# The final norm of the first 704 tokens: token tiles by transposes, or feature rows as they lie

## The chip, the cores and the metric

The kernel runs on one core of a Trainium2 chip. The metric is the device time of one execution in microseconds (us); the kernel before has a median of 1601.08 us over 3 runs (1600.66 to 1601.70).

## The reference

One layer of a streaming encoder on 1,024 prompt tokens and 32 sample tokens of 1,024 features: attention and an mLSTM, a merge, an output projection, a SwiGLU FFN, then the final norm. Only its end matters here:

```python
def rmsnorm(x, g):
    xf = x.astype(jnp.float32)
    y = xf * lax.rsqrt(jnp.mean(xf * xf, axis=-1, keepdims=True) + EPS)
    return (y * g.astype(jnp.float32)).astype(x.dtype)
...
    g, up = jnp.split(h2 @ w_gate_up, 2, axis=-1)
    x = x + gt2 * ((jax.nn.silu(g) * up) @ w_down)
...
    y_prompt = rmsnorm(xp, g_final)
    y_sample = rmsnorm(xs, g_final)
```

## The kernel before, in words

All 1,056 tokens (1,024 and 32) are treated together, with features on partitions and tokens along the free dimension, in three tiles of 352 tokens. The residual `x2[j]` (j = 0 to 7) holds 128 features of all tokens; `cut` = 704 is where the third tile begins. TensorE multiplies in split precision: each weight and each activation is a high and a low part (`split_to`: ScalarE copies the high part, line 409, VectorE or GpSimd subtracts to get the low part, line 410), and every product takes three matmuls (`PASSES`).

The down projection of the FFN comes last. For the first 704 tokens it is finished first, by direct products and a seven-product scheme (line 2057 and `times`, line 1811); its sums lie in `cs[0]` to `cs[7]`. What follows is the loop over j at the end of the kernel: for each j the down projection of the third tile, 22 pieces k in three blocks of 8, 8 and 6, three matmuls for each k, so 66 matmuls (line 2214) in one PSUM bank; then VectorE adds the result to `x2[j][:, 704:]` (line 2224).

The weights come through `Weights`: three raw buffers filled by DMA on SyncE's queue (line 419), and four split buffers `wsp` of 4 pieces each. When TensorE starts a block, the split of the next block is issued; its ScalarE copy waits until TensorE has left the buffer it goes to. The pieces of the third tile are split the same way from `sl` buffers (`split`, issued by `beside` and, where j = 0 needs them, in the loop itself), the last ones while j = 0 runs.

Beside the loop runs a side job, the generator `finish_some`: `Side.tick` is called after every second k, and takes 15 steps over 75 ticks; before j = 7 the job is drained. Its first eight steps add the branch to the residual of the first 704 tokens (VectorE, line 2186, 128x704 each). Then come six token tiles (five of 128 tokens and one of 64), `Finish`: eight TensorE transposes into two PSUM banks (line 2118), two ScalarE squares with a row sum (line 2119), three small GpSimd operations for the inverse root (lines 2126 to 2128), two VectorE multiplications by the inverse root and the gain row `gB` out of PSUM (line 2134), and two DMAs (line 2138) that store 128x512 each.

The last 352 tokens are `End`: three token tiles (128, 128 and 96). `End.ahead` transposes j = 0 to 6 inside j = 7, and `End.last` the remaining one behind it, scales, and stores the left half from ScalarE's queue and the right half from SyncE's. The third tile holds 64 prompt tokens and 32 sample tokens, which go to two outputs, so it takes two DMAs on each queue (line 2182).

The order on TensorE, ScalarE, VectorE and GpSimd is the order in which the program issues the instructions; each engine works through its own list. A scheduler places only SyncE's DMAs.

Of the kernel before, what the change touches and what calls it, by code (L numbers as in the profile page):

```python
# [8 lines left out]
F32 = mybir.dt.float32  # L9
F32R = mybir.dt.float32r  # L10
BF16 = mybir.dt.bfloat16
AF = mybir.ActivationFunctionType
# [127 lines left out]
def hybrid_stream_step(  # L140
# [3 lines left out]
    params, c_rows, w_ada, w_mod, w_in, b_if, rel_row, w_br_att, w_br_mlstm, w_out, w_gate_up, w_down, g_final,  # L144
    y_prompt, y_sample, new_k_p, new_v_p, new_conv_p, new_C_p, new_n_p, new_m_p,
# [1954 lines left out]
    class Finish:  # L2100


        def __init__(self, a, b):
            self.a, self.b, self.py = a, b, (bank(512), bank(512))
            self.st = sl_pool[0].tile([P, 4], F32, tag="fst", name=nm("fst"), bufs=4)
            self.y = tmpt((P, D))
            self.parts = 0

        def take(self, j0, j1):

            n = self.b - self.a
            for h in range(2):
                a, b = max(j0, 4 * h), min(j1, 4 * h + 4)
                if a >= b:
                    continue
                py = self.py[h]
                for j in range(a, b):
                    pe.transpose(py[:n, (j - 4 * h) * P:(j - 4 * h + 1) * P], x2[j][:, self.a:self.b], ident)
                act.activation(self.y[:n, a * P:b * P], py[:n, (a - 4 * h) * P:(b - 4 * h) * P], AF.Square,  # L2119
                               accum_out=self.st[:n, self.parts:self.parts + 1])  # L2120
                self.parts += 1

        def scale(self):
            n, st = self.b - self.a, self.st
            for i in range(1, self.parts):
                pool.tensor_tensor(st[:n, 0:1], st[:n, 0:1], st[:n, i:i + 1], op=ALU.add)  # L2126
            pool.tensor_scalar(st[:n, 0:1], st[:n, 0:1], 1.0 / D, EPS, op0=ALU.mult, op1=ALU.add)
            pool.tensor_tensor(st[:n, 3:4], st[:n, 0:1], mhalf[:n, 0:1], op=ALU.pow)

        def put(self):  # L2130
            n, y = self.b - self.a, self.y
            for h in range(2):
                cs = slice(h * 512, (h + 1) * 512)
                dve.scalar_tensor_tensor(y[:n, cs], self.py[h][:n], self.st[:n, 3:4], gB[:n, cs],
                                         op0=ALU.mult, op1=ALU.mult)
                for q, u, v in col_segments(self.a, self.b):
                    out = y_sample[0, u - S:v - S] if q else y_prompt[0, u:v]
                    sp.dma_start(out[:, cs], y[u - self.a:v - self.a, cs])

    class End:  # L2140
# [28 lines left out]
        def last(self):  # L2169
# [5 lines left out]
            for i, (y, py, (a, b)) in enumerate(zip(self.ys, self.py, self.cuts)):  # L2175
# [3 lines left out]
                for eng, cs in ((act, slice(0, 512)), (sp, slice(512, D))):  # L2179
                    for q, u, v in col_segments(a, b):  # L2180
                        out = y_sample[0, u - S:v - S] if q else y_prompt[0, u:v]
                        eng.dma_start(out[:, cs], y[u - a:v - a, cs])

    def finish_some(ranges):
        for j in range(KD):
            dve.scalar_tensor_tensor(x2[j][:, :cut], cs[j], gt2[:, 0, j:j + 1], x2[j][:, :cut],
                                     op0=ALU.mult, op1=ALU.add)
            yield
        last = None
        for a, b in ranges:  # L2190
            x = Finish(a, b)
            x.take(0, KD)
            x.scale()
            if last:
                last.put()
            last = x
            yield
        last.put()
# [83 lines left out]
```

## Time and profile before

| | |
|---|---|
| median of 3 runs | 1601.08 us |
| the profiled execution's own time | 1600.87 us |
| its span in the trace | 1598.5 us |
| instructions in the span | 27336 |
| busy: TensorE, VectorE, ScalarE, GpSimd | 98%, 70%, 50%, 26% |
| stores of the six token tiles (line 2138) | 12 DMAs of 256 KB, the last issued at 1575.6 us |

The span is what the trace covers; the execution's time is 2.37 us longer. In the profile, PE is TensorE's matmuls, PEld its weight loads, DVE VectorE, ACT ScalarE, POOL GpSimd, SPq and ACTq the DMA queues of SyncE and ScalarE; L2214 is line 2214 of the kernel. The chain of waits is followed back from the last instruction: its rows have a start, a duration, and the engine that was worked on or waited for. Rows of the timeline have a start, a duration, engine, line, operation and tiles, and in brackets the idle time ahead and what ended it.

### The profile page before, as it was taken

To read this page: it belongs to the slowest core of one execution; us is meant where nothing else is said; L and a number is where in the kernel's file an instruction comes from. 1 tells how busy PE (TensorE), PEld (TensorE's weight loads), DVE (VectorE), ACT (ScalarE), POOL (GpSimd) and SP (SyncE) were. 2 spreads that over 40 slices of the span, in tenths; PEclk is the share of its full clock that TensorE was granted. 3 is DMA by queue.
4 is the path that set the end of the run, shared out by engine and by line. 5 is a ranking of instruction groups with operands and counts; after the bars stand their busy time and mean duration, and the time that the engine had idled before them with its cause. 6 is when DMAs were issued, how large, how long until landed. Compare 5 with 4: busy or idle time off the path is not lost.

```text
span 1598.5 us, 27336 instructions
## 1 busy us (share of the span) xinstructions
PE 1569.2 (98%) x10197; PEld 1549.3 (97%) x10197; DVE 1122.9 (70%) x2285; ACT 791.3 (50%) x1749; POOL 423.3 (26%) x450
## 2 busy tenths in 40 slices
PE   7999999999999999999999999999999999999997
PEld 6999999999999999999999999999999999999997
DVE  7766555556766845546655699898898986799754
ACT  3665463544555545444434655544445444544443
POOL 1343242433223311000012100675565650000001
PEclk9999999999999999999999999999999999999999
DMA  9823223343132332775453311223222237427454
GB/s 362 268 81 97 94 83 108 91 137 109 36 97 65 87 86 87 127 257 174 130 152 113 96 55 59 89 67 105 70 88 86 68 94 240 136 80 251 137 153 127
DMA packets 209906, 193.48 MB, mean 121 GB/s; under 512 B 11483, under 2 KB 179071, under 8 KB 208751
## 3 DMA queue, kind: packets, MB, share of 16 engines
q1 hardware_dynamic: 207214, 189.92, 38.7%
q10 hardware_dynamic: 2528, 1.77, 0.4%
q8 instruction: 80, 1.31, 0.4%
q14 instruction: 52, 0.42, 0.1%
q0 software_dynamic: 32, 0.06, 0.0%
HBM read 153.24 MB, written 41.63 MB: 122 GB/s over the span
## 4 chain that ended last, share of the span: by engine, by line
PE 91%; DVE 3%; DMA 2%; ACT 2%; issue 1%; SPq 0%; POOL 0%; ACTq 0%; DVEq 0%; POOLq 0%
PE mm L443 41%; PE psb L1811 18%; PE mm L1811 10%; PE mm L2214 3%; PE mm L878 3%; PE psb L2214 2%; PE psV L783 2%; PE psb L2057 2%; PE psS L725 2%; DMA s<-in_w_ada_dram 1%; PE psT L752 1%; PE mm L2057 1%; DMA t<-in_x_sample_dram 1%; PE psV L1112 1%; PE mm L475 1%
## 5 line engine op out<-in xcount | busy, mean ns | idle before, releaser
L443 PE MATMUL mm<-s,wsp 128*128 128x352 f32 x4104 | 687.0, 324 | 0.1
L443 PEld LDWEIGHTS mm<-s,wsp 128*128 128x128 f32 x4104 | 657.3, 188 | 1.8 <-issue 0.4
L410 DVE TENSOR_TENSOR wsp<-wraw,wsp 128x512 fp32r<-128x512 f32 (+1 forms) x280 | 235.6, 858 | 127.4 <-ACT wsp L409 125.3
L1811 PE MATMUL psb<-s,wsp 128*128 128x352 f32 x1611 | 271.7, 322 | 1.6 <-DVE wsp L410 0.9
L409 ACT ACTIVATE wsp<-wraw 128x512 fp32r<-128x512 f32 x336 | 199.5, 617 | 139.0 <-PE psb L1811 42.4
L1811 PEld LDWEIGHTS psb<-s,wsp 128*128 128x128 f32 x1611 | 260.5, 188 | 2.1 <-DVE wsp L410 1.1
L1811 PE MATMUL mm<-s,wsp 128*128 128x352 f32 x933 | 159.3, 322 | 0.0
L1811 PEld LDWEIGHTS mm<-s,wsp 128*128 128x128 f32 x933 | 151.2, 188 | 0.5 <-DVE wsp L410 0.5
L745 POOL TENSOR_SCALAR st<-st,mx 128x640 f32<-128x640 f32 (+5 forms) x72 | 53.1, 738 | 186.3 <-DVE mx L744 168.3
L1207 DVE CUSTOM_DVE_ANT_0 junk<-wa,t 128x512 bf16<-128x512 f32 x128 | 94.9, 742 | 2.8 <-DMA wa<-in_w_mod_dram 1.8
L410 POOL TENSOR_TENSOR wsp<-wraw,wsp 128x512 fp32r<-128x512 f32 x56 | 74.1, 1343 | 58.2 <-ACT wsp L409 56.8
L739 DVE CUSTOM_DVE_ANT_0 st<-psS,bias 128x640 f32<-128x640 f32 (+5 forms) x72 | 44.5, 618 | 57.1 <-PE psS L725 41.9
L740 ACT ACTIVATE st<-st,mx 128x640 f32<-128x640 f32 (+5 forms) x72 | 47.9, 666 | 63.2 <-DVE mx L739 62.1
L1758 POOL TENSOR_TENSOR t<-t,sl 128x352 f32<-128x352 f32 x19 | 18.4, 968 | 213.1 <-ACT sl L1756 213.1
L759 ACT ACTIVATE pT<-psT 128x640 fp32r<-128x640 f32 (+3 forms) x80 | 38.7, 493 | 62.6 <-PE psT L752 47.5
L2126 POOL TENSOR_TENSOR fst<-fst 128x1 f32<-128x1 f32 (+1 forms) x6 | 1.2, 192 | 236.7 <-ACT t L2119 236.7
L764 DVE TENSOR_TENSOR pT<-psT,pT 128x640 fp32r<-128x640 f32 (+3 forms) x80 | 44.0, 558 | 22.2 <-ACT pT L759 22.2
L1420 POOL TENSOR_TENSOR wraw<-wraw,raw 128x512 f32<-128x512 f32 x33 | 55.8, 1704 | 0.9
L878 PE MATMUL mm<-s,s 128*128 128x264 f32 (+3 forms) x432 | 54.5, 283 | 0.0
L2214 PE MATMUL mm<-s,wsp 128*128 128x352 f32 x330 | 54.4, 324 | 0.0
L2214 PEld LDWEIGHTS mm<-s,wsp 128*128 128x128 f32 x330 | 53.0, 188 | 0.0
L878 PEld LDWEIGHTS mm<-s,s 128*128 128x128 f32 (+1 forms) x432 | 52.0, 179 | 0.5
(369 smaller groups left out, 2482.2 us busy)
## 6 DMA issues: line engine op xcount, KB each, us to landing
wraw<-in_w_in_dram SPq DMA_DIRECT2D x38, 512.0 KB, 4.0
wraw<-in_w_gate_up_dram SPq DMA_DIRECT2D x33, 512.0 KB, 3.9
wa<-in_w_mod_dram SPq DMA_DIRECT2D x64, 256.0 KB, 2.8
wraw<-in_w_down_dram SPq DMA_DIRECT2D x32, 512.0 KB, 4.1
a_d<-t SPq DMA_DIRECT2D x22, 528.0 KB, 2.7
g_d<-t SPq DMA_DIRECT2D x16, 528.0 KB, 3.7
x<-xres SPq DMA_DIRECT2D x16, 528.0 KB, 8.6
t<-g_d SPq DMA_DIRECT2D x16, 528.0 KB, 4.5
```

The source lines that it names most:

```text
L409: act.activation(dst[:, 0], src, AF.Copy)
L410: eng.tensor_tensor(dst[:, 1], src, f(dst[:, 0]), op=ALU.subtract)
L443: pe.matmul(pt[:, :hi - lo], wt[(w0 + k) // 4][:, a, (w0 + k) % 4], xt[k][:, b, lo:hi], start=(k == 0 and q == 0), stop=(k == n - 1 and q ...
L739: dve.tensor_tensor_reduce(so, sv, bi, -1.0, 3.0e38, ALU.add, ALU.min, mx[:n, 1:2])
L740: act.activation(st[:n, :w], st[:n, :w], AF.Exp, bias=mx[:n, 1:2], scale=-1.0, accum_out=mx[:n, 2:3])
L745: pool.tensor_scalar(st[:n, :w], st[:n, :w], mx[:n, 3:4], 1.0, op0=ALU.mult, op1=ALU.mult)
L878: pe.matmul(pt[:n, :wd], hs[k][:, a, i * P:i * P + n], whl[b][:, k, :wd], start=(k == 0 and q == 0), stop=(k == KD - 1 and q == 2))
L1207: dve.tensor_tensor_reduce(junk, wa, crow[:, c], 1.0, 0.0, ALU.mult, ALU.add, at)
L1420: self.eng.tensor_tensor(a(dst), a(x), a(y), op=op)
L1811: pe.matmul(acc, wt[:, a, k], x[k][:, b], start=(start and not onto and k == 0 and q == 0), stop=(stop and k == 3 and q == 2), skip_group_ ...
L2057: pe.matmul(acc, wt[k // 4][:, u, k % 4], piece_of[k, i][:, v], start=(k == 0 and q == 0), stop=(k == KP - 1 and q == 2))
L2214: pe.matmul(acc, wt[(k - k0) // 4][:, u, (k - k0) % 4], piece_of[k, 2][:, v], start=(k == 0 and q == 0), stop=(k == NF - 1 and q == 2))
```

## The change

The first 704 tokens are no longer turned into token tiles. The side job adds the branch to the residual as before, squares each `x2[j][:, :704]` on ScalarE, and adds the squares up on VectorE into one 128x704 tile `known`. Six matmuls with a column of ones (line 2163 of the changed kernel) give the sums of each token's row; VectorE scales them, GpSimd takes the power, and `bcast_cols` (line 242, six transposes of a broadcast column and two ScalarE copies) spreads the inverse roots over all partitions as `rb`. Eight VectorE operations of 128x704 multiply `x2[j]` by the gain column and `rb` in place, and each is stored as it lies by one DMA to a new output `y_rows` (8, 128, 704), which the host turns. The third tile's 352 tokens go to one output `y_end`, so that `End`'s last token tile takes one DMA on each queue. The gain is loaded as columns too (`gcols`, 128x8). The side job has 28 steps over 80 ticks.

```diff
-    class Finish:
...
-                for j in range(a, b):
-                    pe.transpose(py[:n, (j - 4 * h) * P:(j - 4 * h + 1) * P], x2[j][:, self.a:self.b], ident)
-                act.activation(self.y[:n, a * P:b * P], py[:n, (a - 4 * h) * P:(b - 4 * h) * P], AF.Square,
-                               accum_out=self.st[:n, self.parts:self.parts + 1])
...
                 for eng, cs in ((act, slice(0, 512)), (sp, slice(512, D))):
-                    for q, u, v in col_segments(a, b):
-                        out = y_sample[0, u - S:v - S] if q else y_prompt[0, u:v]
-                        eng.dma_start(out[:, cs], y[u - a:v - a, cs])
+                    eng.dma_start(y_end[a - cut:b - cut, cs], y[:n, cs])
-    def finish_some(ranges):
+    def finish_some():
+        known, rb = tmpt(), tmpt()
         for j in range(KD):
+            x = x2[j][:, :cut]
+            dve.scalar_tensor_tensor(x, cs[j], gt2[:, 0, j:j + 1], x, op0=ALU.mult, op1=ALU.add)
             yield
+            if j == 0:
+                act.activation(known[:, :cut], x, AF.Square)
+            else:
+                sq = tmpt()
+                act.activation(sq[:, :cut], x, AF.Square)
+                yield
+                dve.tensor_tensor(known[:, :cut], known[:, :cut], sq[:, :cut], op=ALU.add)
+        yield
+        yield
+        pt = bank(8)
...
+        for i, (a, b) in enumerate(subs):
+            pe.matmul(pt[:b - a, i:i + 1], known[:, a:b], ones[:, 0:1], start=True, stop=True)
+        for n, u, v in ((P, 0, whole), (cut - whole * P, whole, len(subs))):
+            dve.tensor_scalar(rs[:n, 0, u:v], pt[:n, u:v], 1.0 / D, EPS, op0=ALU.mult, op1=ALU.add)
+        pool.tensor_tensor(rs[:, 1, :6], rs[:, 0, :6], mhalf[:, :6], op=ALU.pow)
+        yield
+        yield
+        bcast_cols(rb, rs[:, 1], [b - a for a, b in subs], 0)
+        yield
+        for j in range(KD):
+            x = x2[j][:, :cut]
+            dve.scalar_tensor_tensor(x, x, gcols[:, j:j + 1], rb[:, :cut], op0=ALU.mult, op1=ALU.mult)
+            sp.dma_start(y_rows[j], x)
             yield
-        last.put()
...
-    job = side.start(finish_some([(a, min(a + P, cut)) for a in range(0, cut, P)]), 15, 75)
+    gcols = sl_pool[0].tile([P, KD], F32, tag="gcols", name="gcols", bufs=1)
+    sp.dma_start(gcols, g_cols)
+    job = side.start(finish_some(), 28, 80)
```

Line 2186 becomes 2146, 2214 becomes 2193, 2224 becomes 2203, 2156 becomes 2116, and 2182 becomes 2140 in the changed kernel.

On TensorE, before, in j = 4, one token tile's transposes stand between two runs of the down projection (psb_16254 is the bank of j = 4, x_1780 to x_1783 the residual, two j in each):

```order
L2214 MATMUL psb_16254<-s_9573,wsp_16226 128x352 x3
L2118 MATMUL psb_16269<-ident,x_1780_14005 128x128
L2118 MATMUL psb_16269<-ident,x_1781_14006 128x128
L2118 MATMUL psb_16269<-ident,x_1782_14007 128x128
L2118 MATMUL psb_16269<-ident,x_1783_14008 128x128
L2118 MATMUL psb_16270<-ident,x_1780_14005 128x128
L2118 MATMUL psb_16270<-ident,x_1781_14006 128x128
L2118 MATMUL psb_16270<-ident,x_1782_14007 128x128
L2118 MATMUL psb_16270<-ident,x_1783_14008 128x128
L2214 MATMUL psb_16254<-s_10003,wsp_16226 128x352 x6
```

Six such groups, 48 transposes, stand in j = 4 to 6; none is left. On TensorE now, at the end of the second block of j = 4 (psb_16279 is its bank, t_15885 the tile `known`, psb_16345 the bank of the sums):

```order
L2193 MATMUL psb_16279<-s_10014,wsp_16281 128x352 x6
L2193 MATMUL psb_16279<-s_10064,wsp_16281 128x352 x6
L2163 MATMUL psb_16345<-ones,t_15885 128x1 x5
L2163 MATMUL psb_16345<-ones,t_15885 64x1
L2193 MATMUL psb_16279<-s_10064,wsp_16313 128x352 x3
L2193 MATMUL psb_16279<-s_9336,wsp_16313 128x352 x3
```

The six column sums follow k = 15 of j = 4. The other new place on TensorE is in j = 5 (psb_16385 is its bank, fst_16346 the inverse roots):

```order
L2193 MATMUL psb_16385<-s_10295,wsp_16358 128x352 x3
L2193 MATMUL psb_16385<-s_10139,wsp_16358 128x352 x3
L242 MATMUL mm_16412<-ident,fst_16346 128x128 x4
L242 MATMUL mm_16418<-ident,fst_16346 128x128
L242 MATMUL mm_16418<-ident,fst_16346 128x64
L2193 MATMUL psb_16385<-s_10003,wsp_16358 128x352 x3
L2193 MATMUL psb_16385<-s_10139,wsp_16358 128x352 x3
```

Six matmuls of k = 16 to 21 of j = 4 and six of k = 0 to 5 of j = 5, each three times, stand between the two places. On VectorE, before, while j = 0 runs (s_10064 to s_9478 are the last six pieces of the third tile, k = 16 to 21):

```order
L410 TENSOR_TENSOR wsp_15889<-wraw_15784,wsp_15889 128x512
L410 TENSOR_TENSOR wsp_15890<-wraw_15784,wsp_15890 128x256
L2186 SCALAR_TENSOR_TENSOR x_1780_14005<-s_14237,amod_293,x_1780_14005 128x704
L410 TENSOR_TENSOR s_10064<-sl_15741,s_10064 128x352
L410 TENSOR_TENSOR s_9336<-sl_15847,s_9336 128x352
L410 TENSOR_TENSOR s_9368<-sl_15851,s_9368 128x352
L410 TENSOR_TENSOR s_9406<-sl_15915,s_9406 128x352
L410 TENSOR_TENSOR wsp_15936<-wraw_15818,wsp_15936 128x512
L410 TENSOR_TENSOR wsp_15937<-wraw_15818,wsp_15937 128x512
L410 TENSOR_TENSOR s_9434<-sl_15922,s_9434 128x352
L410 TENSOR_TENSOR s_9478<-sl_15929,s_9478 128x352
L2186 SCALAR_TENSOR_TENSOR x_1781_14006<-s_14237,amod_293,x_1781_14006 128x704
```

And on VectorE now, at the same place:

```order
L2146 SCALAR_TENSOR_TENSOR x_1780_14005<-s_14237,amod_293,x_1780_14005 128x704
L410 TENSOR_TENSOR wsp_15894<-wraw_15784,wsp_15894 128x512
L410 TENSOR_TENSOR wsp_15895<-wraw_15784,wsp_15895 128x256
L2146 SCALAR_TENSOR_TENSOR x_1781_14006<-s_14237,amod_293,x_1781_14006 128x704
L410 TENSOR_TENSOR s_10064<-sl_15741,s_10064 128x352
L410 TENSOR_TENSOR s_9336<-sl_15847,s_9336 128x352
L410 TENSOR_TENSOR s_9368<-sl_15851,s_9368 128x352
L410 TENSOR_TENSOR s_9406<-sl_15921,s_9406 128x352
L410 TENSOR_TENSOR wsp_15942<-wraw_15818,wsp_15942 128x512
L410 TENSOR_TENSOR wsp_15943<-wraw_15818,wsp_15943 128x512
L410 TENSOR_TENSOR s_9434<-sl_15928,s_9434 128x352
L410 TENSOR_TENSOR s_9478<-sl_15935,s_9478 128x352
```

Both residual steps have moved up: the first ahead of the split of the third weight block, the second ahead of the pieces k = 16 to 21. On ScalarE the first square stands behind the copy for wsp_15895 and ahead of the copies of those six pieces; the second square stands behind them.

More of the change, by code (lines that the diff above doesn't have):

```diff
@@ L2098, in hybrid_stream_step @@
     last()
-    class Finish:
[L2103 to L2116, printed above, removed]
-                for j in range(a, b):
-                    pe.transpose(py[:n, (j - 4 * h) * P:(j - 4 * h + 1) * P], x2[j][:, self.a:self.b], ident)
-                act.activation(self.y[:n, a * P:b * P], py[:n, (a - 4 * h) * P:(b - 4 * h) * P], AF.Square,
-                               accum_out=self.st[:n, self.parts:self.parts + 1])
[L2121 to L2136, printed above, removed]
-                    out = y_sample[0, u - S:v - S] if q else y_prompt[0, u:v]
-                    sp.dma_start(out[:, cs], y[u - self.a:v - self.a, cs])
     class End:
@@ L2188, in finish_some @@
             yield
[L2189 to L2194, printed above, removed]
-                last.put()
-            last = x
+            if j == 0:
[5 more added lines that the diff above has]
+                dve.tensor_tensor(known[:, :cut], known[:, :cut], sq[:, :cut], op=ALU.add)
@@ new lines, in finish_some @@
+        yield
+        yield
+        pt = bank(8)
+        rs = sl_pool[0].tile([P, 2, 8], F32, tag="fst", name=nm("fst"), bufs=1)
+        dve.memset(rs[:, 0], 1.0)
+        subs = [(a, min(a + P, cut)) for a in range(0, cut, P)]
+        whole = cut // P
+        for i, (a, b) in enumerate(subs):
+            pe.matmul(pt[:b - a, i:i + 1], known[:, a:b], ones[:, 0:1], start=True, stop=True)
+        for n, u, v in ((P, 0, whole), (cut - whole * P, whole, len(subs))):
+            dve.tensor_scalar(rs[:n, 0, u:v], pt[:n, u:v], 1.0 / D, EPS, op0=ALU.mult, op1=ALU.add)
@@ L2256 @@
             a = _np.asarray(inputs["w_ada"])[0, :, 2 * D:].reshape(2, 512, 4 * KD, P).transpose(0, 2, 3, 1)
+        elif name == "g_cols":
+            a = _np.asarray(inputs["g_final"]).reshape(KD, P).T
         else:
@@ L2280 @@
         outs[i] = _np.ascontiguousarray(outs[i].transpose(1, 2, 0)).reshape(1, 1, 3, D)
+    rows, end = outs[:2]
+    y = _np.concatenate([rows.reshape(D, 2 * NT).T, end])
+    outs[:2] = [_np.ascontiguousarray(y[None, :S]), _np.ascontiguousarray(y[None, S:])]
     return tuple(outs)
```

12 lines of the change are left out of this document (4 added, 8 removed).

## The prediction

> **What bounds the kernel now.** First the page: who is busy.
>
> ```profile
> span 1598.5 us, 27336 instructions
> PE 1569.2 (98%) x10197; PEld 1549.3 (97%) x10197; DVE 1122.9 (70%) x2285; ACT 791.3 (50%) x1749; POOL 423.3 (26%) x450
> ```
>
> TensorE is busy nearly throughout. A share of the whole span doesn't say what holds the end, so next comes the chain of waits over the last 100 us, where the change lies (start, duration, work, count).
>
> ```profile
> 1538.63 0.97 PE psb L2214 x6
> 1539.60 0.87 PE psb L2118 x8
> 1540.47 4.82 PE psb L2214 x30
> ...
> 1568.11 0.87 PE mm L2118 x8
> 1568.98 6.75 PE psb L2214 x42
> ```
>
> The chain is TensorE alone up to the last residual. The down projection takes 4.82/30 = 6.75/42 = 0.161 us for each matmul, and every group of eight transposes of line 2118 stands in the chain with 0.87 us: nothing else covers it. The timeline confirms this from another side. It shows when VectorE can add the result of j, which is when TensorE has finished j (j = 2, 3 and 6):
>
> ```profile
> 1528.06 0.71 DVE L2224 SCALAR_TENSOR_TENSOR x<-mm,amod,x 128x320 f32<-128x320 f32 x2 [1.54 <-PE mm L2214]
> 1538.67 0.71 DVE L2224 SCALAR_TENSOR_TENSOR x<-mm,amod,x 128x320 f32<-128x320 f32 x2 [1.54 <-PE mm L2214]
> 1575.77 0.71 DVE L2224 SCALAR_TENSOR_TENSOR x<-psb,amod,x 128x320 f32<-128x320 f32 x2 [0.23 <-PE psb L2214]
> ```
>
> Without transposes j = 3 takes 10.61 us. j = 4 to 6 take 37.10 us, where three times 10.61 is 31.83; the six groups therefore cost 5.27 us, or 0.88 each.
>
> **The change, part by part.** *Removed on TensorE:* 6 groups, 5.22 us by the chain and 5.27 us by the timeline. I take 5.25. The squares, GpSimd's small operations, VectorE's multiplications and the stores of these tiles lie beside TensorE and give nothing when they go.
>
> *Added on TensorE:* six column sums and six broadcast transposes. The second norm of the layer has both kinds; its three column sums and, elsewhere, six of them and three broadcasts stand in the chain like this:
>
> ```profile
> 839.93 0.51 PE psV L1581 x6
> ```
>
> ```profile
> 894.95 0.12 PE psV L1581 x2
> 895.07 0.22 PE psV L1583 x2
> ...
> 895.91 0.17 PE psV L1583 x2
> 896.08 4.92 PE mm L443 x30
> 900.99 0.30 PE mm L242 x3
> 901.30 2.91 PE mm L443 x18
> ```
>
> A column sum leaves two records of a matmul, 0.22 us together for 128 tokens and 0.17 for 96. Six of them last from 894.95 to 896.08, 1.13 us, and the matmuls behind them take 0.09 us more than 30 times 0.161. By the other row three take 0.51, so six 1.02. The change has five of 128 tokens and one of 64: 5 x 0.22 and about 0.12, 1.2 us (between 1.0 and 1.3). Three broadcasts take 0.30 us, so six 0.60 (up to 0.65). Together 1.8 us.
>
> The Trainium skill, page "TensorE: Matmul & The Clock Gate", section "LDWEIGHTS (loading the stationary operand)", says that loading the stationary operand costs by its columns, not by its rows or by what is then multiplied. It speaks against this change: a sum that multiplies one single column still loads a whole tile. By its P/1.2 ns, 128 columns are 0.107 us, so an estimate from it is 2 x 0.107 for each of five sums, half of that for the sum of 64 tokens, and 0.107 for each of six broadcasts: 1.81 us, and a net of 3.44. The trace agrees with it (0.22 us for the two records of a sum).
>
> *Net on TensorE:* 5.25 - 1.8 = 3.4 us less, between 3.2 and 3.7.
>
> *Does VectorE and ScalarE's new work stay beside it?* These are the rows for j = 3 to the end (busy, mean ns; idle ahead and its cause), and one square and one residual step:
>
> ```profile
> L410 DVE TENSOR_TENSOR wsp<-wraw,wsp 128x512 fp32r<-128x512 f32 x23 | 15.3, 688 | 15.7 <-ACT wsp L409 15.5
> L409 ACT ACTIVATE wsp<-wraw 128x512 fp32r<-128x512 f32 x23 | 14.3, 632 | 12.8 <-PE mm L2214 7.4 <-PE psb L2214 3.7 <-DVE wsp L410 1.3
> ```
>
> ```profile
> L2186 DVE SCALAR_TENSOR_TENSOR x<-s,amod,x x8: 943/945/949, 1500.9 to 1532.7; 128x704 f32<-128x704 f32 x8
> ```
>
> ```profile
> L1756 ACT ACTIVATE sl<-x 128x352 f32<-128x352 f32 x21 | 10.5, 498 | 38.8 <-DVE x L1750 36.5 <-DVE rs L1578 2.2
> ```
>
> In the split of the weights VectorE waits for ScalarE and ScalarE waits for TensorE to leave a buffer: the split runs as early as its buffers allow. From that moment the first half of a block needs 0.63 + 0.69, about 1.4 us with handovers, and TensorE comes to it after the block in between, 24 matmuls or 3.9 us, or 18 and 2.9 us behind the third block of a j. The slack is 2.5 and 1.5 us. Neither new operation has a row of its size: a square of 128x704 lies between the 0.50 of half the width and its double, 1.0, and I take 0.9; the sum of two 128x704 tiles has one operand less than the residual step, so at most 0.95 and at least its half, and I take 0.9. A step of sum and next residual is then 1.85 us on VectorE; split of a block 1.4 and this step come to 3.25, under 3.9. The order puts such a step into the first and the second block of a j and none into the third, so it has 3.9 us each time. The square follows one step of the job later, 2.86 ticks of 6 matmuls, 2.8 us, when its residual is long done. I charge nothing for it; the cover is the slack of 1.5 us, and a step that were wholly late would cost what exceeds it. The eight last multiplications (0.95 each, in steps of their own) fall under the same cover. Every store is behind its own multiplication on SyncE's queue, ahead of a weight load that waits for a later VectorE instruction anyway; in bytes the stores are the same.
>
> The narrowest place is in j = 0, where the last pieces (k = 20, 21) are split just ahead of TensorE:
>
> ```profile
> 1496.06 10.75 PE L2214 MATMUL psb<-s,wsp 128*128 128x352 f32 x66
> ...
> 1498.85 0.69 DVE L410 TENSOR_TENSOR wsp<-wraw,wsp 128x512 fp32r<-128x512 f32 x1 [0.87 <-ACT wsp L409]
> ...
> 1500.90 0.95 DVE L2186 SCALAR_TENSOR_TENSOR x<-s,amod,x 128x704 f32<-128x704 f32 x1
> ...
> 1503.95 0.63 ACT L409 ACTIVATE wsp<-wraw 128x512 fp32r<-128x512 f32 x1 [1.29 <-PE psb L2214]
> ...
> 1504.61 0.69 DVE L410 TENSOR_TENSOR wsp<-wraw,wsp 128x512 fp32r<-128x512 f32 x1 [0.42 <-ACT wsp L409]
> 1505.22 0.95 DVE L410 TENSOR_TENSOR s<-sl,s 128x352 fp32r<-128x352 f32 x2
> ```
>
> The low part of k = 20 is done at 1505.70; TensorE needs it for its 63rd matmul, at 1496.06 + 62 x 0.161 = 1506.04. Only 0.3 us are free. But what holds it is the ScalarE copy at 1503.95, which TensorE's buffer releases. The new first square (0.9) goes into ScalarE's 1.29 us of waiting ahead of that copy, and the first residual step moves up into VectorE's 0.87 us of waiting ahead of 1498.85; its place at 1500.90 goes to the second one. So the time of that copy stays, with 0.4 us left on ScalarE. If the square took 1.4 us, TensorE would stand for some 0.1 us.
>
> *The sums' way to the broadcast:* behind the column sums VectorE scales them and GpSimd takes the power, then TensorE broadcasts. GpSimd's power had these times at its longest and VectorE's scaling this one:
>
> ```profile
> 1570.51 1.03 POOL L2128 TENSOR_TENSOR fst<-fst,mhalf 64x1 f32<-64x1 f32 x1
> 840.47 0.22 DVE L1586 TENSOR_SCALAR rs<-psV 96x1 f32<-96x1 f32 x2 [2.78 <-PE psV L1581]
> ```
>
> 1.3 us plus handovers, against 36 matmuls, 5.8 us, that the order puts in between. VectorE's scaling waits for TensorE with the split of the next j queued behind it; it waits about 0.7 us into a block whose split has 1.5 us of slack. Nothing is charged.
>
> *The end:* the last token tile saves one DMA on each of two queues. Before:
>
> ```profile
> 1593.89 1.00 SPq L2182 DMA_DIRECT2D out_dram<-t  x1
> 1594.21 1.18 ACTq L2182 DMA_DIRECT2D out_dram<-t  x2
> ```
>
> ```profile
> 1594.50:1595.00 0.50, 0.00 (x0) 0.00 (x0) 0.00 (x0) 0.00 (x0) 0.00 (x0) 0.50 1.03 385
> 1595.50:1596.00 0.50, 0.00 (x0) 0.00 (x0) 0.00 (x0) 0.00 (x0) 0.00 (x0) 0.50 1.02 266
> 1597.00:1597.25 0.25, 0.00 (x0) 0.00 (x0) 0.00 (x0) 0.00 (x0) 0.00 (x0) 0.50 0.04 8
> ```
>
> The last two columns are the DMA share and GB/s. The last issue would end about 0.6 us earlier on ScalarE's queue (half of 1.18), but the transfer engines are full until 1597.0, so the data may set the end and not the issue. The gain is between 0 and 0.6 us; since the rate falls to 266 GB/s when the small last DMAs run, I take 0.3. The Trainium skill, page "DMA: Bandwidth & Descriptors", section "Specifications", gives about 358 GB/s to the memory for a core, by which data alone would set this end and the gain be near 0; this trace shows 385 GB/s, above that figure.
>
> **The sum:** -5.25 + 1.8 - 0.3 = -3.7 us. The profiled execution took 1600.87 us (span 1598.5 and 2.37 around it), 0.21 below the median of 1601.08; so 1597.2 in its terms and **1597.4 us** for the median.
>
> **The rivals.**
>
> *Slower: the split starves.* ScalarE and VectorE take their lists in order. If a square came to ScalarE before its residual step was done, the copies behind it would wait, and residual, square and sum (0.95 + 0.9 + 0.9) would stand in a row ahead of a split: 2.75 + 1.4 = 4.1 us against 2.9 behind a third block, TensorE 1.2 us late. Seven sums would give 8.4 us, and 1601.1 - 3.7 + 8.4 = 1605.8. It decides once these three run as one and eat over 1.5 us. For it speaks that VectorE is at 70% already; against it that the order holds them a step apart and keeps them out of the third block.
>
> *A new wait at the handovers.* TensorE would wait at the column sums for the last sum, or at the broadcast for the power. If the way took 2 us longer than the 1.3 it would still be covered; with two waits of about 1 us each, net -1.7, 1599.4.
>
> *The transposes were free.* Had the 48 transposes hidden under loads, only the added work would count: +1.8 - 0.3, 1602.6. The 10.61 us of j = 3 against 37.10/3 of j = 4 to 6 speak against it.
>
> **How the numbers follow.** My forecast has a chance of 0.74; its own range is -3.2 - 0 to -3.7 - 0.6, so 1596.8 to 1597.9 us, with half a microsecond of scatter between runs (1600.66 to 1601.70) below. The waits at the handovers, or another partial loss of up to 2 us, get 0.16; the starved split 0.07; free transposes 0.03. The range 1596.3 to 1599.4 holds the forecast and most of the partial losses, about 8 in 10. 0.2% is 3.2 us, about what a measurement here can tell from no change, and my forecast lies only just beyond: of its 0.74 I count 0.70 as faster by over 0.2%, and 0.04 as within; with the partial losses, the free transposes and 0.01 for a split that starves only once or twice that makes 0.24. The other 0.06 of the starved split are slower.
>
> **What would show it.** Right: the chain of the changed kernel is again TensorE alone; j without added work takes 10.61 us; j = 4 about 11.8 and j = 5 about 11.2; j = 6 10.6; line 2163 stands with about 1.2 us and line 242 with 0.6; the last store is issued some 0.6 us sooner after the last residual. Wrong: TensorE idle ahead of a matmul of line 2193 released by VectorE's or ScalarE's `wsp`, in j = 0 released by the pieces, or ahead of line 2163 or 242; a j of over 10.7 us without added work; an end that takes as long behind the last matmul as before.

## The result, and the profile after

| | before | changed |
|---|---|---|
| median of 22 runs each | 1601.78 us | 1599.12 us |
| lowest to highest | 1600.55 to 1603.17 | 1597.14 to 1600.75 |
| profiled execution: own time, span | 1600.87, 1598.5 us | 1597.75, 1596.1 us |
| residual of j = 0 to that of j = 7 | 81.73 us | 78.95 us |
| last residual to the end of the span | 9.86 us | 10.31 us |

The last row is taken from the span of the trace (1598.54 and 1596.05 us), which the page rounds to 0.1 us. The ratio of the times is 0.9982, 95% interval 0.9975 to 0.9988: 2.9 us faster, between 1.9 and 4.0 (the medians lie 2.7 us apart). The forecast was 3.7 us. The whole range of the ratio is below 1, but only part of it beyond the 0.2% of the prediction. The busy times on the page of the changed kernel:

```profile
PE 1566.1 (98%) x10167; PEld 1546.2 (97%) x10167; DVE 1126.4 (71%) x2291; ACT 790.5 (50%) x1735; POOL 420.0 (26%) x433
```

VectorE's total grew by 3.5 us and TensorE's fell by 3.1. As before, what counts is the chain at the end. The chain of waits of the changed kernel (start, duration, work, count):

```profile
1496.15 10.60 PE psb L2193 x66
1506.75 31.81 PE mm L2193 x198
1538.57 7.71 PE psb L2193 x48
1546.27 1.21 PE psb L2163 x12
1547.49 6.02 PE psb L2193 x36
1553.50 0.74 PE mm L242 x6
1554.25 22.39 PE psb L2193 x138
...
1578.92 6.79 PE psb L2193 x42
1585.72 0.02 issue
1585.74 0.56 DVE x L2203
```

It is TensorE alone again, without a gap, up to the last residual. The six groups of transposes are gone; lines 2163 and 242 stand in their place with 1.21 and 0.74 us. The 36 matmuls between them take 6.02 us, where 36 times 0.1607 (31.81/198) is 5.79: some of the cost of the new places is booked on the matmuls behind them. So the timeline is the better measure; its rows give VectorE's residual of the third tile, that is the end of j = 3 to 6:

```profile
1538.60 0.71 DVE L2203 SCALAR_TENSOR_TENSOR x<-mm,amod,x 128x320 f32<-128x320 f32 x2 [1.48 <-PE mm L2193]
1550.63 0.71 DVE L2203 SCALAR_TENSOR_TENSOR x<-psb,amod,x 128x320 f32<-128x320 f32 x2 [1.69 <-PE psb L2193]
1562.20 0.71 DVE L2203 SCALAR_TENSOR_TENSOR x<-psb,amod,x 128x320 f32<-128x320 f32 x2 [0.68 <-PE psb L2193]
1572.80 0.71 DVE L2203 SCALAR_TENSOR_TENSOR x<-psb,amod,x 128x320 f32<-128x320 f32 x2 [0.68 <-PE psb L2193]
```

j = 4, 5 and 6 take 12.03, 11.57 and 10.60 us, 34.20 together against 37.10 before. Against a j without extra work (10.61) the column sums cost 1.42 us and the broadcasts 0.96. TensorE's waits over the last 106 us are these two, each of which the kernel before has with the same length (columns: total, times, longest):

```profile
PE psb L1811 <- ACT wsp L409: 0.7, 1, 0.7
PE mm L2116 <- DVE x L2203: 0.6, 1, 0.6
```

So no split of weights, no piece, no sum and no power is waited for. The second part of the result lies behind the last residual: from there the first store is issued as soon as before (3.09 us) and the last issue ends 0.84 us sooner (5.87 us against 6.71, both on ScalarE's queue), but the end of the span comes 0.45 us later. SyncE's queue, which ends the program, has one long wait there:

```profile
SPq L2254 <- DMA out_dram<-t: 4.1, 1, 4.1
```

Two theories are thus to be tested. On TensorE: *A*, the small pieces (64 rows or 64 columns) stall TensorE; *B*, each new place has a fixed edge whatever its shapes. At the end: the issue sets it, or the data, or the single larger DMA is itself worse than two. Besides, the largest rival, the starved split, is provoked on purpose.

### The profile page after: what moved, and what is told of

Its sections match the earlier page's. It is cut to its first block, busy times and chain, and to the rows that moved or that the text cites. A ratio compares the mean times of both kernels' runs of the same rounds, so it can differ in the third digit from the quotient of the medians.

```text
span 1596.1 us, 27244 instructions
## 1 busy us (share of the span) xinstructions
PE 1566.1 (98%) x10167; PEld 1546.2 (97%) x10167; DVE 1126.4 (71%) x2291; ACT 790.5 (50%) x1735; POOL 420.0 (26%) x433
## 4 chain that ended last, share of the span: by engine, by line
PE 91%; DVE 3%; ACT 2%; DMA 2%; issue 1%; SPq 0%; POOL 0%; ACTq 0%; DVEq 0%; POOLq 0%
PE mm L443 41%; PE psb L1811 18%; PE mm L1811 11%; PE psb L2193 3%; PE mm L878 3%; PE mm L2193 2%; PE psV L783 2%; PE psb L2057 2%; PE psS L725 2%; PE psT L752 1%; DMA s<-in_w_ada_dram 1%; PE mm L2057 1%; DMA t<-in_x_sample_dram 1%; PE psV L1112 1%; PE mm L475 1%
## 5 line engine op out<-in xcount | busy, mean ns | idle before, releaser
L443 PE MATMUL mm<-s,wsp 128*128 128x352 f32 x4104 | 687.0, 324 | 0.0
L443 PEld LDWEIGHTS mm<-s,wsp 128*128 128x128 f32 x4104 | 657.3, 188 | 1.8 <-issue 0.4
L1811 PE MATMUL psb<-s,wsp 128*128 128x352 f32 x1611 | 271.7, 322 | 1.6 <-DVE wsp L410 0.9
L1811 PEld LDWEIGHTS psb<-s,wsp 128*128 128x128 f32 x1611 | 260.5, 188 | 2.1 <-DVE wsp L410 1.1
L1811 PE MATMUL mm<-s,wsp 128*128 128x352 f32 x933 | 159.3, 322 | 0.0
L1811 PEld LDWEIGHTS mm<-s,wsp 128*128 128x128 f32 x933 | 151.2, 188 | 0.5 <-DVE wsp L410 0.5
L2193 PE MATMUL psb<-s,wsp 128*128 128x352 f32 x330 | 54.2, 324 | 0.0
L2193 PEld LDWEIGHTS psb<-s,wsp 128*128 128x128 f32 x330 | 53.1, 188 | 0.1
```

The source lines that it names most:

```text
L443: pe.matmul(pt[:, :hi - lo], wt[(w0 + k) // 4][:, a, (w0 + k) % 4], xt[k][:, b, lo:hi], start=(k == 0 and q == 0), stop=(k == n - 1 and q ...
L1811: pe.matmul(acc, wt[:, a, k], x[k][:, b], start=(start and not onto and k == 0 and q == 0), stop=(stop and k == 3 and q == 2), skip_group_ ...
L2193: pe.matmul(acc, wt[(k - k0) // 4][:, u, (k - k0) % 4], piece_of[k, 2][:, v], start=(k == 0 and q == 0), stop=(k == NF - 1 and q == 2))
```

## The experiments

The times that serve here are mostly read inside the profile (one j lasts the same within 0.01 us from profile to profile), since a median of whole executions is uncertain by about 1 us.

**The price of the work on TensorE.** `e5_no_pe` takes all twelve small operations away:

```diff
-        for i, (a, b) in enumerate(subs):
-            pe.matmul(pt[:b - a, i:i + 1], known[:, a:b], ones[:, 0:1], start=True, stop=True)
...
-            dve.tensor_scalar(rs[:n, 0, u:v], pt[:n, u:v], 1.0 / D, EPS, op0=ALU.mult, op1=ALU.add)
+            dve.tensor_scalar(rs[:n, 0, u:v], known[:n, u:v], 1.0 / D, EPS, op0=ALU.mult, op1=ALU.add)
...
-        bcast_cols(rb, rs[:, 1], [b - a for a, b in subs], 0)
+        for u, v in ((0, 512), (512, cut)):
+            act.activation(rb[:, u:v], known[:, u:v], AF.Copy)
```

> Leaves out the six column sums and the six broadcasts on TensorE: the scaling and the two ScalarE copies take columns of the sum of squares instead, so VectorE, ScalarE and GpSimd do the same number of operations of the same sizes; the stored values of the first 704 tokens are not normalized. Theory A (the added work costs the sum of the rows of the kernel before, as forecast): the last residual comes 1.8 us earlier than in the changed kernel. Theory B (it costs 1.4 + 0.96 as j = 4 and 5 measure): 2.4 us earlier, and j = 4 and j = 5 take 10.6 us each.

Every j from 1 to 6 took 10.60 to 10.61 us, and j = 0 to j = 7 76.57 us, 2.38 less than in the changed kernel. Its chain has nothing between the matmuls from 1539.38 on:

```profile
1539.38 35.69 PE psb L2192 x222
```

222 matmuls in 35.69 us are 0.1608 each. The added work costs 2.4 us, not 1.8, and everything that stayed on the other engines costs nothing.

**Stall or edge.** `e1_full_rows` gives the sixth broadcast 128 rows instead of 64:

```diff
-        bcast_cols(rb, rs[:, 1], [b - a for a, b in subs], 0)
+        bcast_cols(rb, rs[:, 1], [P] * len(subs), 0)
```

> The sixth broadcast takes 128 rows of the inverse roots instead of 64, so the six of line 242 have one shape. Changed kernel: j = 5 lasted 11.57 us where 10.61 is that of a j without extra work, so the broadcasts cost 0.96 where 0.6 was forecast. Theory A (TensorE stalls where the shape of the loaded operand changes; the timeline has 0.17 us ahead of the load of the 64-row piece): j = 5 takes 11.3 to 11.4 us. Theory B (going from the down projection to small matmuls and back costs a fixed edge, whatever the shape): j = 5 stays at 11.55 to 11.65 us. j = 4 stays at 12.0 by both.

j = 5 took 11.31 us, 0.26 less; j = 4 12.02. Theory A's number. The reason stands in the weight loads. In the changed kernel:

```profile
1553.18 0.62 PEld L242 LDWEIGHTS mm<-ident,fst 128*128 128x128 f32 x5
1553.98 0.13 PEld L242 LDWEIGHTS mm<-ident,fst 64*128 64x128 f32 x1 [0.17 <-issue]
```

With 128 rows for all six:

```profile
1554.94 0.73 PEld L242 LDWEIGHTS mm<-ident,fst 128*128 128x128 f32 x6
```

Ahead of the 64-row load the loads stood still for 0.17 us, released by nothing that the profile shows; with six equal loads that gap is gone. A rule of the Trainium skill, page "TensorE: Matmul & The Clock Gate", section "LDWEIGHTS (loading the stationary operand)", bears on it: a load of few rows takes as long as one of 128. For the load itself the trace agrees (0.13 and 0.62/5 us). But the place with the 64-row load was the dearer one, by 0.26 us; the page's rule leaves that out, and the measurement decides.

`e8_full_tiles` does the same for the sums as well: 64 columns of zeros fill up `known`, and the sixth sum loads 128 columns.

```diff
+        pool.memset(known[:, cut:6 * P], 0.0)
...
-        subs = [(a, min(a + P, cut)) for a in range(0, cut, P)]
+        subs = [(a, a + P) for a in range(0, cut, P)]
```

> The sum of squares is filled up with 64 columns of zeros, so that the sixth column sum loads 128 columns like the others, and the sixth broadcast takes 128 rows; one scaling instead of two. Theory A (a change of shape stalls TensorE): the sums lose a stall and gain 0.1 us for 64 more columns, j = 4 takes 11.9 to 12.05 us, j = 5 11.3 to 11.4. Theory B (a fixed edge at each of the two places): j = 4 12.1, j = 5 11.55 to 11.65.

j = 4 took 11.95 us (0.08 less, though it loads 64 columns more) and j = 5 11.24. Its chain:

```profile
1547.72 1.23 PE psb L2163 x12
1548.95 5.89 PE psb L2193 x36
1554.85 0.66 PE mm L242 x6
1555.50 22.18 PE psb L2193 x138
```

The matmuls behind the sums went from 6.02 to 5.89 us, those behind the broadcasts from 22.39 to 22.18. Theory A holds for both places. With full tiles the broadcasts cost 0.63 us in all, the forecast's 0.60 to 0.65, and the sums 1.34: in the trace the loads of a full sum start 0.112 us apart, two for each sum, so six sums are 12 x 0.112, and no edge is left over. In the changed kernel the first load of 64 columns starts 0.206 us behind the load ahead of it, the second 0.055 later, and the load after that 0.151 later; so the 64-column sum costs 0.08 us more than a full one, 0.30 us against 0.22. Why j = 5 is another 0.07 shorter here than in `e1_full_rows`, with the same broadcasts, was not found out.

**The work twice.** `e9_twice` makes the six sums twice in a row, and then the six broadcasts:

```diff
-        for i, (a, b) in enumerate(subs):
+        for i, (a, b) in list(enumerate(subs)) * 2:
...
         bcast_cols(rb, rs[:, 1], [b - a for a, b in subs], 0)
+        bcast_cols(rb, rs[:, 1], [b - a for a, b in subs], 0)
```

> The six column sums are made twice in a row, and the six broadcasts (with their two ScalarE copies) twice. In the changed kernel j = 4 takes 12.03 us and j = 5 11.57, 1.42 and 0.96 above a j without extra work. Theory A (the pieces cost more than forecast, the 64-row and 64-column ones above all, so the second set costs as much as the first): j = 4 13.4 and j = 5 12.5 us. Theory B (the pieces cost what was forecast, 1.2 and 0.6, and the rest is an edge paid once): j = 4 13.2 and j = 5 12.2 us.

j = 5 took 12.42 us: a second set of broadcasts costs 0.85, nearly as much as the first, since it too has its 64-row load. But j = 4 took 14.96 us, 2.93 more than with one set, far from both theories. The chain had the 24 records of the sums with 2.62 us, 1.41 more than the 12; the rest came behind them, and the windows show why (last three columns: granted clock, DMA share, GB/s; the number in brackets counts every instruction that touches the window):

```profile
1550.00:1551.00 1.00, 1.00 (x6) 1.00 (x6) 0.96 (x4) 0.00 (x0) 0.66 (x1) 0.65 0.00 0
1551.00:1552.00 1.00, 1.00 (x5) 1.00 (x5) 0.46 (x1) 0.00 (x0) 1.00 (x1) 0.50 0.00 0
1552.00:1553.00 1.00, 1.00 (x5) 1.00 (x4) 0.00 (x0) 0.00 (x0) 0.71 (x2) 0.50 0.37 102
1553.00:1554.00 1.00, 1.00 (x6) 1.00 (x6) 0.00 (x0) 0.44 (x1) 0.00 (x0) 0.64 0.89 257
1554.00:1555.00 1.00, 1.00 (x8) 1.00 (x8) 0.33 (x1) 0.53 (x2) 0.00 (x0) 1.00 0.58 169
```

TensorE is busy all the time, but the granted clock is 0.5 from 1550.31 to 1553.72 us, 3.41 us. Inside that stretch the matmuls of the down projection start 0.293 us apart in the trace, instead of 0.161, so it holds 11.6 of them instead of 21.2, and 9.6 x 0.161 = 1.54 us are lost. With the 1.41 us of the second set this makes 2.95, against 2.93 measured. So the second set costs as much as the first: theory A's price of 13.4 us for j = 4, and the fall of the clock on top.

Was the fall of the clock chance? `e12_twice_again` is the same kernel once more:

> Column sums and broadcasts made twice, once more, to see whether the granted clock of 0.5 for some 3.3 us behind the doubled sums comes again. Theory A (2.8 us of matmuls of one column count as a pause for the clock, and it falls in some or all executions): j = 4 takes 14.9 us again in the profile, or 13.2 in an execution where it stays up; the times lie 3.8 us above those of the changed kernel or spread down to 2 us above. Theory B (it was chance, unconnected with the doubling): j = 4 takes 13.2 to 13.3 us and the times lie 2.1 us above the changed kernel.

j = 4 took 14.96 us again, at a clock of 0.56 and 0.59 over 1550 to 1554 us, and the median of 10 runs was 1602.94 us (1601.48 to 1604.92), 3.8 us above that of the changed kernel. That is what theory A says. `e13_twice_apart` makes the sums twice as well, but the second lot a step of the job later (and the broadcasts once):

```diff
+        for n in range(2):
             for i, (a, b) in enumerate(subs):
                 pe.matmul(pt[:b - a, i:i + 1], known[:, a:b], ones[:, 0:1], start=True, stop=True)
+            if n == 0:
+                yield
...
-    job = side.start(finish_some(), 28, 80)
+    job = side.start(finish_some(), 29, 80)
```

> The column sums are made twice, but the second six one step of the side job later, some 18 matmuls of the down projection behind the first (29 steps over 80 ticks); the broadcasts once. Doubled in a row, the sums were followed by 3.3 us at a granted clock of 0.5 in both profiles. Theory A (it is the length of the uninterrupted run of one-column matmuls, 2.8 us, that counts as a pause): no stretch at 0.5 after the sums; the two lots cost 1.4 us each, so from the residual of j = 3 to that of j = 6 34.2 + 1.4 = 35.6 us, and the times lie 1.4 us above the changed kernel, 0.9 to 1.9 below the kernel before. Theory B (it is their number within some microseconds): the clock falls again, 37.3 us.

The chain of `e13_twice_apart`:

```profile
1545.95 1.21 PE psb L2164 x12
1547.16 3.10 PE psb L2196 x18
1550.26 1.21 PE psb L2164 x12
1551.48 5.03 PE psb L2196 x30
```

The clock stayed at 1.00 throughout, j = 4 took 13.42 us, j = 4 to 6 together 35.60: the number of theory A. Its median over 10 runs was 1599.84 us, ratio to the kernel before 0.9984 (0.9975 to 0.9994): 1.0 to 4.0 us below it, where theory A had 0.9 to 1.9. So 2.8 us of one-column matmuls in a row brought the clock down in both profiles, and 1.4 us in none of those of the changed kernel and its variants, nor did two lots with 3.1 us between. That the length of the run alone decides is not shown by this; the last section has more on it.

**The end.** Three edits. `e2_end_two` stores the last token tile in two DMAs of 64 and 32 rows again:

```diff
-                    eng.dma_start(y_end[a - cut:b - cut, cs], y[:n, cs])
+                    for q, u, v in col_segments(a, b):
+                        eng.dma_start(y_end[u - cut:v - cut, cs], y[u - a:v - a, cs])
```

> The last token tile is stored in two DMAs of 64 and 32 rows on each queue again, everything else as in the changed kernel. From the last residual to the end of the span the kernel before took 9.82 us, the changed one 10.36. Theory A (the issue of the DMAs sets the end, as the forecast had it for half of the step): 0.3 to 0.6 us longer than in the changed kernel, 10.7 to 11.0. Theory B (the data sets the end, the number of issues doesn't matter): 10.4, give or take what profiles differ by. Theory C (a single larger DMA ends later than two small ones): 9.8.

`e7_before_one_output` is the kernel before with the one DMA alone (its `Finish` and `End` store to two outputs, of 704 and of 352 tokens):

```diff
-                    for q, u, v in col_segments(a, b):
-                        out = y_sample[0, u - S:v - S] if q else y_prompt[0, u:v]
-                        eng.dma_start(out[:, cs], y[u - a:v - a, cs])
+                    eng.dma_start(y_end[a - cut:b - cut, cs], y[:n, cs])
```

> The kernel before with one part of the change alone: the first 704 tokens go to one output and the last 352 to another, both still as token tiles, so that the last token tile takes one DMA on each queue. Theory A (the issue sets the end): the stretch from the last residual to the end, 9.82 us in the kernel before, becomes 9.2 to 9.5. Theory B (the data sets it): 9.8, give or take what profiles differ by. Theory C (a single DMA of 96 rows ends later than two of 64 and 32): 10.3.

`e3_end_half` leaves ScalarE's three stores out:

```diff
-                for eng, cs in ((act, slice(0, 512)), (sp, slice(512, D))):
+                for eng, cs in ((sp, slice(512, D)),):
```

> Leaves out the stores of the left half of the last 352 tokens (0.72 MB, the three DMAs on ScalarE's queue); the right half is stored as in the changed kernel. Theory A (the issue sets the end; the last issue on SyncE's queue stays where it was): the stretch from the last residual to the end, 10.36 us in the changed kernel, shrinks by 0.3 us at most. Theory B (the data sets the end): 0.72 MB less at 270 to 389 GB/s is 1.9 to 2.7 us less; since the transfers of the other queue start late, 1.2 to 2.7 us less.

From the last residual to the end, in all profiles (the two kernels with full tiles and two or three DMAs come below; the changed kernel and its variants whose end is the same in code are in one row). The expectations had taken 9.82 and 10.36 from the page's rounded spans; the table goes by those of the trace:

| end of the kernel | last residual to end |
|---|---|
| before, two DMAs on each queue | 9.86 us |
| before, one (`e7_before_one_output`) | 10.10 |
| changed, one (and `e1`, `e4`, `e5`, `e8`, `e9`, `e12`, `e13`) | 10.31 (10.31, 10.30, 10.31, 10.32, 10.32, 10.32, 10.32) |
| changed, two (`e2_end_two`) | 10.04 |
| full tiles, two (`e10_full_two`) | 9.99 |
| full tiles, three (`e11_full_three`) | 10.02 |
| changed, right half alone (`e3_end_half`) | 7.68 |

With half the data the end came 2.63 us sooner. With it went ScalarE's last issue, which had ended 0.85 us behind SyncE's, so at most that much of the 2.63 can be the issue's; and the changed kernel itself ended its issues 0.84 us sooner than the one before and gained nothing. The data sets the end, as theory B of that run says. But merging the DMAs is not without effect: in both kernels it makes the end later, by 0.24 us before and 0.27 after. That is theory C, though with a quarter of a microsecond instead of the 0.5 that it was given. Some windows of the changed kernel, of half a microsecond, the first 6.5 us behind its last residual:

```profile
1592.24:1592.74 0.50, 0.00 (x0) 0.00 (x0) 0.00 (x0) 0.00 (x0) 0.00 (x0) 0.50 0.97 254
...
1593.24:1593.74 0.50, 0.00 (x0) 0.00 (x0) 0.00 (x0) 0.00 (x0) 0.00 (x0) 0.50 0.94 311
1593.74:1594.24 0.50, 0.00 (x0) 0.00 (x0) 0.00 (x0) 0.00 (x0) 0.00 (x0) 0.50 0.43 160
1594.24:1594.74 0.50, 0.00 (x0) 0.00 (x0) 0.00 (x0) 0.00 (x0) 0.00 (x0) 0.50 0.08 29
```

The same stretches of `e2_end_two`, which follow a residual 1.47 us later:

```profile
1593.71:1594.21 0.50, 0.00 (x0) 0.00 (x0) 0.00 (x0) 0.00 (x0) 0.00 (x0) 0.50 1.03 295
...
1594.71:1595.21 0.50, 0.00 (x0) 0.00 (x0) 0.00 (x0) 0.00 (x0) 0.00 (x0) 0.50 0.84 197
1595.21:1595.71 0.50, 0.00 (x0) 0.00 (x0) 0.00 (x0) 0.00 (x0) 0.00 (x0) 0.50 0.61 222
1595.71:1596.21 0.50, 0.00 (x0) 0.00 (x0) 0.00 (x0) 0.00 (x0) 0.00 (x0) 0.50 0.00 0
```

The rate is lower there with both. But with one DMA the transfer engines fall idle one after another (share 0.43, then 0.08), with two the share drops to zero at once. The last large packet of the stores ends 8.76 us behind the last residual with one DMA and 8.38 with two; in the kernel before it is 8.74 with one and 8.42 with two. Why a DMA of 96 rows ends so unevenly no run shows. Another 0.2 us separate the changed kernel from the one before with the same number of DMAs (10.04 against 9.86, 10.31 against 10.10). The data ends at the same time there, so they arise behind it; from what stays open.

**The starved split, on purpose.** `e4_one_step` issues residual, square and sum of a j in one step:

```diff
             dve.scalar_tensor_tensor(x, cs[j], gt2[:, 0, j:j + 1], x, op0=ALU.mult, op1=ALU.add)
-            yield
...
                 act.activation(sq[:, :cut], x, AF.Square)
-                yield
                 dve.tensor_tensor(known[:, :cut], known[:, :cut], sq[:, :cut], op=ALU.add)
+            yield
...
-    job = side.start(finish_some(), 28, 80)
+    job = side.start(finish_some(), 21, 80)
```

> Residual, square and sum of a j are issued in one step of the side job (21 steps over 80 ticks instead of 28). VectorE's sum then waits for ScalarE's square, and the weight split is queued behind it: 0.95 + 0.78 + 0.89 and a split of 1.4 make 4.0 us in a row, against 3.9 us of cover in the first and second block of a j and 2.9 behind a third. Theory A (the forecast's reckoning of the slack holds): TensorE waits for wsp at up to seven places, 0.1 us in the middle of a j and 1.1 us behind a third block; last residual 1 to 8 us later than in the changed kernel. Theory B (the slack is larger than reckoned, the order of the steps is of no weight): last residual within 0.3 us.

The waits of TensorE's matmuls, beside the two that the changed kernel has too:

```profile
PE psb L2192 <- DVE s L410: 0.6, 1, 0.6
PE psb L2192 <- ACT s L409: 0.3, 1, 0.3
```

and the timeline around the end of j = 0:

```profile
1505.34 0.89 DVE L2152 TENSOR_TENSOR t<-t,t 128x704 f32<-128x704 f32 x1 [0.86 <-ACT t L2151]
1506.14 1.29 DVE L410 TENSOR_TENSOR wsp<-wraw,wsp 128x512 fp32r<-128x512 f32 x2
...
1506.78 0.59 PE L2192 MATMUL psb<-s,wsp 128*128 128x352 f32 x2 [0.31 <-ACT s L409]
...
1507.35 0.96 DVE L410 TENSOR_TENSOR s<-sl,s 128x352 fp32r<-128x352 f32 x2
1507.92 0.92 PE L2192 MATMUL psb<-s,wsp 128*128 128x352 f32 x4 [0.55 <-DVE s L410]
```

VectorE stands 0.86 us for the square, the split of a block is behind it, and the pieces k = 20 and 21 come 1.5 us later, counted from the first matmul of j = 0, than in the kernel before (10.67 us against 9.16): TensorE waits 0.31 and 0.55 us, and j = 0 lasts 12.0 us instead of 10.6. That is the narrowest place of the prediction. In j = 1 to 3 VectorE pauses for the squares alone (0.86 to 0.92 us each), its residual of the third tile comes up to 2.7 us late (j = 1 and 2 are 1.27 and 1.39 us longer by its rows; j = 3, which has the column sums in this kernel, is 0.96 shorter than a j without them). TensorE waits for `wsp` only once there, with a weight load early in j = 3:

```profile
1534.10 2.06 PEld L2192 LDWEIGHTS mm<-s,wsp 128*128 128x128 f32 x13 [0.33 <-DVE wsp L410]
```

From the first matmul of j = 0 to the last residual it is 91.41 us against 89.75, 1.66 us more: 1.4 in j = 0 and 0.3 in j = 3. That is inside the "1 to 8" of theory A, but most of it at another place than it said, and at one of its seven places instead of all. The median was 1600.48 us, ratio to the kernel before 0.999 (0.9981 to 1.0).

**Both finds together.** `e10_full_two` has the full tiles of `e8_full_tiles` and the two DMAs of `e2_end_two`; `e11_full_three` has three DMAs of 32 rows instead:

```diff
-                    eng.dma_start(y_end[a - cut:b - cut, cs], y[:n, cs])
+                    for u, v in ((0, n),) if n == P else ((0, 32), (32, 64), (64, 96)):
+                        eng.dma_start(y_end[a + u - cut:a + v - cut, cs], y[u:v, cs])
```

> Both finds in one kernel: full tiles for the column sums and broadcasts, and the last token tile stored in two DMAs on each queue. Theory (the stalls of the small pieces and the uneven end of the single DMA are separate and add): from the residual of j = 0 to that of j = 7 78.55 us (changed kernel 78.95), from the last residual to the end 9.9 to 10.0 us (10.36), together 0.7 to 0.8 us less than the changed kernel, whose median is 2.7 us below the kernel before: 3.4 us, a ratio near 0.9979. Rival (the two finds were scatter of single profiles): 78.9 and 10.3.

> As with two DMAs for the last token tile, but three of 32 rows on each queue. Theory A (in a single DMA of 96 rows the transfer engines end unevenly, and smaller DMAs even that out): 9.7 to 10.0 us from the last residual to the end, with the DMA share near 1 until it drops at once. Theory B (two is the best; a third issue of 0.34 us on ScalarE's queue and 0.6 on SyncE's comes on top): 10.2 to 10.6.

`e10_full_two`: 78.55 us from j = 0 to j = 7 and 9.99 us behind the last residual, 0.72 us less than the changed kernel, so the two add. By the times it is the changed kernel's equal: median of 11 runs 1598.62 us, ratio to the kernel before 0.9979 (0.9970 to 0.9988), which overlaps 0.9975 to 0.9988. Three DMAs end as two do (10.02 us): close to theory A's 9.7 to 10.0, but no further gain.

## Why the prediction was right, and where it was not

The place and the sign were right, and 1599.1 us lies in the range of 1596.3 to 1599.4; the predicted gain of 3.7 us (its terms add up to 3.75) was too large. That the range holds the result is in part luck. The span that followed from the forecast's own terms, 1596.8 to 1597.9 us, does not hold it; the range reached further up for waits at the handovers, and no such wait came. On the other side, 0.7 us of the 1.7 us between forecast and result are not the change's: the three runs behind 1601.08 us lay that much below the median of 22. Of the signs that the prediction named, TensorE alone in the chain came true, and so did one of those for being wrong: the end takes no less time than before. Whether the gain is over 0.2%, for which it gave 0.70, stays open: 0.18% was measured. Term by term:

| term | forecast | measured | by |
|---|---|---|---|
| 48 transposes removed | -5.25 us | -5.28 | j = 4 to 6 without extra work, 31.82 us (`e5_no_pe`), against 37.10 |
| six column sums | +1.2 | +1.42 | j = 4 |
| six broadcasts | +0.6 | +0.96 | j = 5 |
| work on VectorE and ScalarE | 0 | 0 | TensorE's waits, `e5_no_pe` |
| handovers between sums and broadcasts | 0 | 0 | TensorE's waits |
| the end | -0.3 | +0.45 | last residual to the end |

With 0.16 us less up to the residual of j = 0 in this pair of profiles, and 0.10 and 0.02 more in j = 1 and 7, the terms give the span's -2.49 us (1598.54 to 1596.05).

*Removed.* The reading that transposes in the chain are covered by nothing was right to 0.03 us.

*Added on TensorE: mis-sized by 0.6 us.* The prediction took the rows of single sums and broadcasts from places where the pieces are nearly all of 128 or 96, and gave the 64-token sum half a price, 0.12 us, and the 64-token broadcast that of a full one. What it left out is the shape. A 64-row load holds TensorE up by 0.26 us (`e1_full_rows`), and the sum with 64 columns cost 0.30 us, more than the 0.22 of one with 128 (`e8_full_tiles`). That is nearly all of the sums' excess: with six full tiles they cost what the prediction's rows give, six times 0.22. Of the broadcasts' excess another 0.07 us went with the full sums, without a known reason.

*VectorE and ScalarE.* The forms that no row had shown, one square, one sum, and the last multiplication (mean ns of one):

```profile
L2173 DVE SCALAR_TENSOR_TENSOR x<-x,gcols,t 128x704 f32<-128x704 f32 x8 | 7.4, 946 | 0.0
L2154 DVE TENSOR_TENSOR t<-t,t 128x704 f32<-128x704 f32 x7 | 6.2, 886 | 0.3 <-ACT t L2152 0.3
L2152 ACT ACTIVATE t<-x 128x704 f32<-128x704 f32 x7 | 5.5, 781 | 5.8 <-DVE x L2146 5.8
```

0.78 and 0.89 us against 0.9 and 0.9, all of it under cover. The rival of the starved split had its mechanism right (a square waited for in VectorE's list holds up what is behind it, `e4_one_step`), but its price of 8.4 us, seven times 1.2, was wrong: in the middle of the loop the lateness is made good before TensorE needs the split but for one wait of 0.33 us, and most of what it costs is paid once, in j = 0, where the prediction had seen 0.3 us of margin.

*The handovers.* The way from sums to broadcast was longer than reckoned:

```profile
1547.82 2.31 POOL L2166 TENSOR_TENSOR fst<-fst,mhalf 128x6 f32<-128x6 f32 x1 [221.07 <-DVE fst L2165]
```

Six columns at once took 2.31 us; the prediction had taken the 1.03 of one column. The 6.0 us of matmuls in between still covered it. So this rival fell because of the distance in the order, not because of the price.

*The end: the sign was wrong.* The step "the data may set the end and not the issue ... I take 0.3" split the difference where one side held: the data sets it (`e3_end_half`). And its supposition that the rate falls "when the small last DMAs run" was mistaken; the rate falls with one DMA as well, and the one DMA ends more raggedly. What the prediction worked out from the section "Specifications" of the Trainium skill's page "DMA: Bandwidth & Descriptors", a gain near 0, was a better guide in this point than the middle taken; the 358 GB/s given there is still below the 385 that the rows of the kernel before show. The 0.27 us that the merged DMA loses, and the 0.2 us behind the data, were in no term.

## What to carry to other kernels

Price a step on TensorE by the lengths of whole stretches with and without it, not by its own rows: part of its cost stands on the matmuls behind it. Fill small pieces up to full tiles where it is cheap; here a piece of 64 rows or 64 columns cost more than a full one. Before merging or splitting the last stores, find out what sets the end by leaving some of the data out: where the data does, fewer issues gain nothing, and how evenly the last DMA spreads over the transfer engines may decide instead.

## What was not expected of the hardware

One-column matmuls count little for the clock. Two lots in a row, 2.8 us in which TensorE is busy by every row of the trace, were followed twice by 3.41 us at a granted clock of 0.5; one lot of 1.4 us, or two lots 3.1 us apart, were not. The Trainium skill, page "TensorE: Matmul & The Clock Gate", section "Part 1: The HAM clock gate (the "warmup" mystery)", has a window of about 3.4 us, free-running, after which an idle TensorE is throttled to half. The length of the slow stretch agrees with that. But here no idle window was needed: a stretch of very short matmuls was enough.

In the traces the clock changes in steps of 3.413 us. Every stretch at 0.5 ahead of the end lasts so long, and the falls of one profile lie a whole number of such steps apart (`e9_twice`: 427.32 and 1550.31 us, 329 steps). What counts is how much TensorE streams within one step, as far as these traces show. In `e9_twice` and `e12_twice_again` the 2.8 us of sums lay wholly inside one step (1546.90 to 1550.31 and 1546.82 to 1550.23 us), and the clock fell at its end. An estimate from the traces, which charges 0.161/352 us for each column that a matmul streams: behind the first 50 us of all 14 profiles, the clock fell after every step in which columns were streamed for at most 0.33 of the time (24 falls, 14 of them at the ends of the kernels), and after none with 0.35 or more. In the first 50 us some steps with less passed, so this is not the whole rule. Nor is it tested by an edit: no run moves the doubled sums against the steps, and by this reading a border in their middle would have spared the clock.

The same fall of the clock stands in single profiles earlier in the kernel, mostly at about 106 or about 428 us. At 428 us it follows a pause of TensorE of about 2 us, which is there in the profile of the changed kernel too, without the fall. The steps fit this: in `e1_full_rows` the pause, 425.6 to 427.6 us, lies inside the step from 424.9 to 428.3; in the changed kernel a border at 425.5 divides it, 425.1 to 427.1. The eight profiles with a fall at one or two of these places or at 41 us (`e1`, `e2`, `e3`, `e8`, `e9`, `e10`, `e12`, `e13`) reach the residual of j = 0 at 1507.74 to 1508.58 us; before, changed, `e5`, `e7` and `e11`, without one there (`e11` has one at 19 us), at 1506.34 to 1507.88; `e4`, without one, is longer in j = 0 by its edit. This goes with a part of the scatter of about 3 us between executions of one kernel, and it is why sub-microsecond questions were read from lengths inside the loop.
